# Summed squares ahead of the norm statistics, and a reordered end, in a two-layer hybrid backbone step on eight cores

## The chip, the cores and the metric

The kernel runs on all 8 cores of one Trainium2 chip, with one program and different data on each core. The metric is the device time of the slowest core in microseconds. In slow runs some cores, mostly of one die, run at a lower granted TensorE clock, and the time is longer.

## The reference

One inference step of a two-layer network. Layer 0 mixes tokens with gated linear attention and a Fourier transform, layer 1 with a chunked gMLP and a short convolution. Each layer has two modulated RMS norms and a squared-ReLU feed-forward. A final RMS norm ends it. Cut to what matters here:

```python
def rmsnorm(x, g):
    xf = x.astype(jnp.float32)
    y = xf * lax.rsqrt(jnp.mean(xf * xf, axis=-1, keepdims=True) + EPS)
    return (y * g.astype(jnp.float32)).astype(x.dtype)

for l in range(DEPTH):                      # DEPTH = 2, D = 1024, D_FF = 4096
    ...                                     # six modulation vectors from the conditioning
    h = rmsnorm(x, norm_mix_g[l]) * (1.0 + sc_m) + sh_m
    y = even_mixer(h, ...) if l % 2 == 0 else odd_mixer(h, ...)
    x = x + g_m * y
    h = rmsnorm(x, norm_ffn_g[l]) * (1.0 + sc_f) + sh_f
    x = x + g_f * (jnp.square(jax.nn.relu(h @ ffn_w1[l])) @ ffn_w2[l])
return rmsnorm(x, final_norm_g), outs_f, outs_b
```

## The kernel before

A core holds 1536 tokens as three blocks of 512: blocks 0 and 1 are one request's latent tokens, block 2 is context. The residual `xT[m]` has the 1024 features as 8 chunks of 128 partitions and the 512 tokens as columns. The mean of squares over features therefore crosses partitions, and it is made on TensorE: each chunk is squared on ScalarE (ACT) and multiplied by a matrix of constants, and eight such matmuls add up in one PSUM bank.

```python
def norm_stats(m, x):
    ps = PT(R)
    for c in range(8):
        sq = ring(sqr)
        act(sq[:], x[:, c, :], AF.Square, [x[:, c, :]], [sq[:]])
        R.add("pe", [(lambda sq=sq, c=c: nc.tensor.matmul(ps.f(), onesb[:], sq[:],
                      start=(c == 0), stop=(c == 7)), [sq[:], onesb[:]], 216)], W=[ps])
    r = ring(rsr)
    act(r[:], lambda: ps.f(), AF.Ln, ...)          # r = exp(-0.5 * ln(mean + eps))
    act(r[:], r[:], AF.Exp, ..., scale=-0.5)
    return r

def norm(l, wh, m):
    r = norm_stats(m, xT[m])
    for c in range(8):
        nt = ring(ntr)
        ...   # VectorE: nt = x * gain * r;  ACT: hT[m][:, c] = nt + shift
```

The second feed-forward product takes its weights in four pieces `u` of two output chunks each. The last pieces run block by block, each block followed by its final norm and eight stores:

```python
    if half == 1:                                   # inside ffn(l, hooks)
        for m in range(NM):
            for u in (2, 3):
                for o2 in range(2):
                    ffn2(l, ws[u], u, o2, m)        # 16 matmuls, then x += gate * psum on VectorE
            yield m
...
for m in ffn(1, lambda k: None):
    r = norm_stats(m, xT[m])
    for c in range(8):
        ys = ring(ysr)                              # 7 buffers of [128, 512]
        ...                                         # VectorE: ys = x * gain * r
        store(y_d[m, c], ys[:], "dys%d" % i, 128 * 2048)
```

Instructions are not issued in the order of this text. The program records them and a list scheduler orders each engine's queue by priority. `bl` is the estimated length of the work that depends on an operation, so an edit at the end changes the order of everything ahead of it:

```python
o.prio = o.seq - 1e7 if o.dma is not None and o.eng == "pool" else 30.0 * o.seq - o.bl
```

```python
wO = [w8("evO%d" % i, wevo_d[i]) for i in range(2)]   # weights of the layer-0 output projection, gpsimd queue
xload(0, "sp", 6, 8)
xload(1, "sp")                                        # reload of block 1's input, sync queue
...
for m in range(NM):                                   # gMLP, layer 1
    ...                                               # projections to u and v, 512 columns each
    for jj in range(4):
        for g in range(4):                            # two matmuls of 128 columns: W_s v, and the bias
            ...
        ...                                           # VectorE: mixc = psum * u
```

## Time and profile before

| Kernel before | us |
|---|---|
| median time, first 4 runs | 1202.56 (1200.47 to 1202.95) |
| span of the slowest core in the profile | 1201.7 |
| TensorE busy | 1120.7 (93%) |
| VectorE / ACT / GpSimd busy | 454.1 / 425.0 / 106.0 |

To compare versions I cut every core's profiled run at two landmarks, the starts of the first and of the last matmul of the second feed-forward product (the groups whose tiles are `aT` and `w_f`). This gives a head, a stretch that TensorE bounds, and a tail, averaged over the eight cores. For the kernel before they are 409.6, 768.6 and 20.5 us.

### The profile page before, as it was taken

How to read it: one execution, taken by the hardware profiler on the slowest of the kernel's cores; microseconds unless marked ns; L12 is line 12 of the kernel's file. 1: busy time of each engine (PE TensorE's matmuls, PEld its weight loads, DVE VectorE, ACT ScalarE, POOL GpSimd, SP SyncE). 2: the span in 40 equal slices, each digit the busy share in tenths (PEclk: the TensorE clock that was granted, in tenths of full speed). 3: DMA queues.
4: the chain of work that ended last, by engine and by line, in shares of the span. 5: the costliest groups of instructions: out<-in, count | busy, mean ns of one | idle time of the engine just before them, and what ended most of it. 6: DMA issues, size and time to landing. Idle time of an engine off the chain costs nothing.

```text
span 1201.7 us, 15088 instructions; the slowest of 8 cores (1195.1 to 1201.7 us)
## 1 busy us (share of the span) xinstructions
PE 1120.7 (93%) x6242; PEld 533.5 (44%) x6242; DVE 454.1 (38%) x894; ACT 425.0 (35%) x764; POOL 106.0 (9%) x193
## 2 busy tenths in 40 slices
PE   2479999979989999999999999999999999999994
PEld 0234555644434444444444444444444444444441
DVE  1248476866532222222223514445522222222226
ACT  2473768535553200122113732243733000232013
POOL 2004144520000000000000000000000000000000
PEclk9989999899989999999999989999999999999998
DMA  9980132898951813356333801035232014420005
GB/s 185 229 160 1 23 75 44 153 225 145 193 102 36 140 36 71 70 106 117 71 58 65 148 1 31 6 71 98 43 55 52 5 31 82 88 41 1 1 1 210
DMA packets 19057, 98.19 MB, mean 82 GB/s; under 512 B 2123, under 2 KB 5451, under 8 KB 9132
## 3 DMA queue, kind: packets, MB, share of 16 engines
q0 software_dynamic: 11312, 82.12, 37.9%
q1 hardware_dynamic: 5372, 13.53, 3.5%
q10 hardware_dynamic: 2304, 1.57, 0.4%
q8 instruction: 49, 0.80, 0.3%
q14 instruction: 20, 0.16, 0.1%
HBM read 165.17 MB, written 7.86 MB: 144 GB/s over the span
## 4 chain that ended last, share of the span: by engine, by line
PE 83%; DMA 6%; DVE 4%; ACT 4%; issue 1%; POOL 1%; ACTq 0%; DVEq 0%; POOLq 0%
PE ps L475 80%; DMA w_evC<-wevc 3%; DMA w_evO<-wevo 3%; ACT hA L485 2%; PE ps L1077 1%; PE ps L583 1%; DVE nt L597 1%; DVE ys L1145 1%; ACT sq L485 1%; ACT rstd L485 0%; DVE RS L834 0%; DVE xT L604 0%; DVE hA L877 0%; ACT relu L485 0%; DVE og L866 0%
## 5 line engine op out<-in xcount | busy, mean ns | idle before, releaser
L475 PE MATMUL ps<-hA,w_f 128*128 128x512 bf16 x1536 | 344.9, 382 | 3.0 <-ACT hA L485 2.8
L475 PE MATMUL ps<-aT,w_f 128*128 128x512 bf16 x1536 | 339.7, 379 | 0.0
L485 ACT ACTIVATE relu<-ps 128x512 bf16<-128x512 f32 x192 | 114.1, 596 | 407.3 <-PE ps L475 407.3
L475 PEld LDWEIGHTS ps<-hA,w_f 128*128 128x128 bf16 x1536 | 150.0, 98 | 187.7 <-ACT hA L485 8.6
L475 PEld LDWEIGHTS ps<-aT,w_f 128*128 128x128 bf16 x1536 | 150.3, 98 | 180.9
L604 DVE SCALAR_TENSOR_TENSOR xT<-ps,modT,xT 128x512 f32<-128x512 f32 x144 | 108.0, 751 | 285.0 <-PE ps L475 284.6
L1008 DVE TENSOR_TENSOR aT<-relu 128x512 bf16<-128x512 bf16 x192 | 81.7, 426 | 254.3 <-ACT relu L485 254.1
L485 ACT ACTIVATE sq<-xT 128x512 bf16<-128x512 f32 x120 | 71.7, 623 | 180.7 <-PE ps L583 113.8
L485 ACT ACTIVATE hA<-nt,modT 128x512 bf16<-128x512 f32 x96 | 65.9, 717 | 39.7 <-DVE nt L597 39.3
L597 DVE SCALAR_TENSOR_TENSOR nt<-xT,gsc,rstd 128x512 f32<-128x512 f32 x96 | 68.3, 751 | 17.6 <-ACT rstd L485 13.7
L475 PE MATMUL ps<-w_vg,hA 128*128 128x512 bf16 x288 | 67.0, 380 | 0.9 <-DVE att L849 0.5
L583 PE MATMUL ps<-sq,ones 128*128 128x512 bf16 x120 | 45.1, 401 | 24.1 <-ACT sq L485 22.5
L497 POOL DMA_DIRECT2D w_f<-wf x32 | 17.0, 531 | 430.1 <-PE ps L475 363.9
L475 PE MATMUL ps<-hA,w_evO 128*128 128x512 bf16 x176 | 43.8, 399 | 5.9 <-DMA w_evO<-wevo 5.9
L475 PE MATMUL ps<-hA,w_qk 128*128 128x512 bf16 x192 | 45.3, 379 | 1.4 <-issue 0.6
L819 POOL TENSOR_SCALAR sprevS<-RS,dec 128x192 bf16<-128x192 f32 x56 | 44.3, 801 | 18.4 <-DVE RS L834 16.9
L475 PEld LDWEIGHTS ps<-w_vg,hA 128*128 128x128 bf16 x288 | 27.0, 98 | 30.4 <-issue 1.4
L497 POOL DMA_DIRECT2D w_ada<-wada x20 | 10.8, 540 | 231.2 <-PE ps L475 224.8
L583 PEld LDWEIGHTS ps<-sq,ones 128*128 128x128 bf16 x120 | 11.6, 98 | 42.4 <-ACT sq L485 19.6
L475 PEld LDWEIGHTS ps<-hA,w_evO 128*128 128x128 bf16 x176 | 17.7, 102 | 27.3 <-DMA w_evO<-wevo 6.4
L475 PEld LDWEIGHTS ps<-hA,w_qk 128*128 128x128 bf16 x192 | 17.7, 98 | 20.6 <-issue 1.1
L485 ACT ACTIVATE t<-ps 128x1024 f32<-128x1024 f32 x24 | 23.9, 1023 | 7.9 <-PE ps L475 7.9
(155 smaller groups left out, 932.2 us busy)
## 6 DMA issues: line engine op xcount, KB each, us to landing
w_f<-wf POOLq DMA_DIRECT2D x32, 1024.0 KB, 8.2
w_ada<-wada POOLq DMA_DIRECT2D x20, 1024.0 KB, 10.1
xT<-x POOLq DMA_DIRECT2D x3, 2048.0 KB, 52.3
y<-ys SPq DMA_DIRECT2D x24, 256.0 KB, 2.8
w_ada_s<-wada POOLq DMA_DIRECT2D x4, 1024.0 KB, 27.8
xT<-x SPq DMA_DIRECT2D x2, 2048.0 KB, 23.7
w_vg<-wev POOLq DMA_DIRECT2D x3, 1024.0 KB, 48.3
w_qk<-wev POOLq DMA_DIRECT2D x2, 1024.0 KB, 46.6
```

Source lines behind the costliest of these rows:

```text
L475: parts.append((lambda view=view, l=l, r=r, i=i, n=n: nc.tensor.matmul(view(), l, r, start=(i == 0), stop=(i == n - 1)), [l, r], max(27.0, ...
L485: R.add("act", [(lambda: nc.scalar.activation(out=o(), in_=i(), func=func, **kw), Rd, dur)], W=W, tab=tab)
L497: R.add(q, [(lambda: h.dma_start(out=dst, in_=src), [], 1000 if q == "pool" else 100)], W=[dst], dma=(key, nbytes), prio=prio)
L583: R.add("pe", [(lambda sq=sq, c=c: nc.tensor.matmul(ps.f(), onesb[:], sq[:], start=(c == 0), stop=(c == 7)), [sq[:], onesb[:]], 216)], W=[ps])
L597: lambda nt=nt, c=c: nc.vector.scalar_tensor_tensor(out=nt[:], in0=x[:, c, :], scalar=gsc[l][:, wh, c, ci:ci + 1], in1=r[:], op0=ALU.mult, ...
L604: lambda: nc.vector.scalar_tensor_tensor(out=x[:, oc, :], in0=ps.f(), scalar=modT[l][:, gch + oc, CI(m):CI(m) + 1], in1=x[:, oc, :], op0=A ...
L819: lambda d=d, j=j, pj=pj: nc.gpsimd.tensor_scalar_mul(sprev(d, j), Rt[d][:], dc[:, d, pj:pj + 1]), eng="pool")
L1008: vop(2, [a], [rl[:]], lambda a=a, rl=rl: nc.vector.tensor_tensor(out=a, in0=rl[:], in1=rl[:], op=ALU.mult))
L1077: parts.append((lambda g=g, l_=l_, r_=r_, i=i, p=p: nc.tensor.matmul(p.f(g * 128, (g + 1) * 128), l_, r_, start=(i == 0), stop=(i == 1)), ...
L1145: lambda ys=ys, c=c, m=m, r=r: nc.vector.scalar_tensor_tensor(out=ys[:], in0=xT[m][:, c, :], scalar=pp[:, PP_GF + c:PP_GF + c + 1], in1=r[ ...
```

## The change

Two intents. First, add the eight squared chunks on engines that are free (three adds on GpSimd, four on VectorE) so that one matmul with the constants replaces eight. This is done in seven norms (layer 0's second norm of block 2, all six of layer 1) and in the final norms. Second, shorten the work after the last matmul: block 1 goes ahead of block 2's last four chunks, these run in two halves of 256 columns, output chunks are stored in pairs, and a `bonus` moves priorities. The diff, cut to its core:

```diff
-            o.prio = ... else 30.0 * o.seq - o.bl
+            o.prio = ... else 30.0 * o.seq - o.bl - o.bonus
@@ norm statistics
+        def sq_sum(m, x, accs, n):
+            af, ab = ring(accs[0]), ring(accs[1])          # fp32 partial sum, bf16 result
+            s0 = sq_chunk(x, 0)
+            for c in range(1, n):
+                s1 = sq_chunk(x, c)
+                acc_add((ab if c == n - 1 else af)[:], (s0 if c == 1 else af)[:], s1[:], "pool" if c < 4 else "dve")
+            return ab
@@
+            if accs is None:
                 ...                                         # eight matmuls, as before
+            else:
+                ab = sq_sum(m, x, accs, 8)
+                mm(ps, [(lambda: ps.f(), [(onesb[:], ab[:])])])
@@
-        norm(0, 1, 2)
+        norm(0, 1, 2, accs0)                                # and accs1 for the six norms of layer 1
@@ order of the last feed-forward matmuls
+            if l == 1:
+                k = "a" if u < 2 and m == 2 else "b" if u >= 2 and m == 1 else ("lo" if lo == 0 else "hi") if ... else None
+                if k:                                       # each stage waits for the one before
+                    stages.setdefault(k, []).append(o)
+                    o.parts[0][1].update(stages.get({"a": "-", "b": "a", "lo": "b", "hi": "lo"}[k], ()))
@@ the end
+            for c in range(0, 8, 2):                        # final(m, r, lo, hi): chunks in pairs
+                ...
+                store(y_d[m, c:c + 2, :, lo:hi]..., "act" if m == 2 and c % 4 else "sp")
@@
+        for lo in (0, 256):
+            hi = lo + 256
+            R.bonus = 10000.0 if lo == 0 else 0.0
+            ps = PT(R)
+            mm(ps, [(... [(onesb[:], ab[:, lo:hi])])], stop=False)   # chunks 0 to 3, summed before
+            for c in range(4, 8):
+                ffn2(1, w2last[c // 2], c // 2, c % 2, 2, lo, hi)
+                ...                                         # square and statistics of this chunk
+            rstd_of(ps, r, lo, hi)
+            R.bonus = 0.0
+            final(2, r, lo, hi)
```

More of the change, by code (lines that the diff above doesn't have):

```diff
@@ L41 @@
     __slots__ = ("eng", "parts", "seq", "prio", "tab", "lat", "dma", "newpt", "pts",
-                 "succ", "npred", "bl", "extt", "tag", "ext", "ready", "start", "fin", "key", "val", "dur")
+                 "bonus", "succ", "npred", "bl", "extt", "tag", "ext", "ready", "start", "fin", "key", "val", "dur")
 class Rec:
@@ L60, in __init__ @@
         self.tag = None
+        self.bonus = 0.0
     def sb(self, name, shape, dt, off):
@@ L98, in add @@
         o.tag = self.tag
+        o.bonus = self.bonus
         o.pts = []
@@ L167, in schedule @@
         for o in ops:
-            o.prio = o.seq - 1e7 if o.dma is not None and o.eng == "pool" else 30.0 * o.seq - o.bl
+            o.prio = o.seq - 1e7 if o.dma is not None and o.eng == "pool" else 30.0 * o.seq - o.bl - o.bonus
         cand = {e: [] for e in self.ENGS}
@@ L467, in is_ps, with mm @@
             return isinstance(a, PT)
-        def mm(p, groups, pre=()):
+        def mm(p, groups, stop=True):
             parts = []
@@ L474, in mm @@
                 for i, (l, r) in enumerate(prs):
-                    parts.append((lambda view=view, l=l, r=r, i=i, n=n: nc.tensor.matmul(view(), l, r, start=(i == 0), stop=(i == n - 1)),
+                    parts.append((lambda view=view, l=l, r=r, i=i, n=n: nc.tensor.matmul(view(), l, r, start=(i == 0), stop=(stop and i == n - 1)),
                                   [l, r], max(27.0, nfree(r) / 2.4 + 2.5)))
@@ L574, in CI, with sq_chunk, acc_add, rstd_of @@
             return 0 if m == 2 else 1
-        def norm_stats(m, x):
+        def sq_chunk(x, c):
+            sq = ring(sqr)
+            act(sq[:], x[:, c, :], AF.Square, [x[:, c, :]], [sq[:]])
+            return sq
+        def acc_add(o_, a_, b_, eng):
+            e_ = nc.gpsimd if eng == "pool" else nc.vector
+            vop(1, [o_], [a_, b_], lambda: e_.tensor_tensor(out=o_, in0=a_, in1=b_, op=ALU.add), eng=eng, pool1=False)
+        def sq_sum(m, x, accs, n):
[5 more added lines that the diff above has]
+            return ab
+        def rstd_of(ps, r, lo, hi):
+            act(r[:, lo:hi], lambda: ps.f(lo, hi), AF.Ln, [ps, cst[:]], [r[:, lo:hi]], tab="nle", bias=cst[:, 0:1])
+            act(r[:, lo:hi], r[:, lo:hi], AF.Exp, [r[:, lo:hi]], [r[:, lo:hi]], tab="nle", scale=-0.5)
+        def norm_stats(m, x, accs=None):
             R.tag = "stats%d" % m
             ps = PT(R)
-            parts = []
-            for c in range(8):
-                sq = ring(sqr)
-                act(sq[:], x[:, c, :], AF.Square, [x[:, c, :]], [sq[:]])
-                R.add("pe", [(lambda sq=sq, c=c: nc.tensor.matmul(ps.f(), onesb[:], sq[:], start=(c == 0), stop=(c == 7)), [sq[:], onesb[:]], 216)], W=[ps])
+            if accs is None:
+                for c in range(8):
+                    sq = sq_chunk(x, c)
+                    R.add("pe", [(lambda sq=sq, c=c: nc.tensor.matmul(ps.f(), onesb[:], sq[:], start=(c == 0), stop=(c == 7)), [sq[:], onesb[:]], 216)], W=[ps])
+            else:
+                ab = sq_sum(m, x, accs, 8)
+                mm(ps, [(lambda: ps.f(), [(onesb[:], ab[:])])])
             r = ring(rsr)
-            act(r[:], lambda: ps.f(), AF.Ln, [ps, cst[:]], [r[:]], tab="nle", bias=cst[:, 0:1])
-            act(r[:], r[:], AF.Exp, [r[:]], [r[:]], tab="nle", scale=-0.5)
+            rstd_of(ps, r, 0, 512)
             return r
-        def norm(l, wh, m):
+        def norm(l, wh, m, accs=None):
             R.tag = "norm%d%d%d" % (l, wh, m)
@@ L592, in norm @@
             shc = 0 if wh == 0 else 24
-            r = norm_stats(m, x)
+            r = norm_stats(m, x, accs)
             for c in range(8):
@@ L599, in norm, with resid @@
                 act(h[:, c, :], nt[:], AF.Identity, [nt[:], modT[l][:, shc + c, :]], [h[:, c, :]], bias=modT[l][:, shc + c, ci:ci + 1])
-        def resid(m, oc, ps, l, gch):
-            x = xT[m]
-            vop(1, [x[:, oc, :]], [ps, x[:, oc, :], modT[l][:, gch + oc, :]],
-                lambda: nc.vector.scalar_tensor_tensor(out=x[:, oc, :], in0=ps.f(), scalar=modT[l][:, gch + oc, CI(m):CI(m) + 1], in1=x[:, oc, :],
+        def resid(m, oc, ps, l, gch, lo=0, hi=512):
+            x = xT[m][:, oc, lo:hi]
+            vop(1, [x], [ps, x, modT[l][:, gch + oc, :]],
+                lambda: nc.vector.scalar_tensor_tensor(out=x, in0=ps.f(lo, hi), scalar=modT[l][:, gch + oc, CI(m):CI(m) + 1], in1=x,
                                                        op0=ALU.mult, op1=ALU.add))
@@ L657, in build @@
         y256 = R.sb("y256", [128, 2, 128], BF16, a_s + 16384)
+        a_t4 = so[0]
         t4 = [R.sb("t4_%d" % i, [128, 1024], F32, ats(4096)) for i in range(4)]
@@ L983, in build @@
         outproj(0, wO, hT, 1)
+        accs0 = ([R.sb("af0_%d" % i, [128, 512], F32, a_t4 + i * 2048) for i in range(2)],
+                 [R.sb("ab0_%d" % i, [128, 512], BF16, a_t4 + 4096 + i * 1024) for i in range(2)])
         norm(0, 1, 0)
@@ L989, in build @@
         norm(0, 1, 1)
-        norm(0, 1, 2)
+        norm(0, 1, 2, accs0)
         aT = [R.sb("aT%d" % m, [128, 16, 512], BF16, a_s + m * 16384) for m in range(NM)]
         a_s2 = a_s + 49152
+        accs1 = ([R.sb("af1_%d" % i, [128, 512], F32, a_s2 + 12288 + i * 2048) for i in range(2)],
+                 [R.sb("ab1", [128, 512], BF16, a_s2 + 16384)])
+        assert a_s2 + 17408 <= s_end
         def ffn(l, hooks):
@@ L1015, in ffn @@
                         for m in range(NM):
+                            R.bonus = 0.0 if half == 0 or l == 0 else 0.0
                             for o2 in range(2):
                                 ffn2(l, w, u, o2, m)
+                        R.bonus = 0.0
                     hooks((half, 1, u))
                 if half == 1:
-                    for m in range(NM):
+                    w2last.update({2: ws[2], 3: ws[3]})
+                    for m in range(NM if l == 0 else 2):
+                        R.bonus = 0.0 if l == 0 else 0.0
                         for u in (2, 3):
@@ L1023, in ffn, with ffn2 @@
                                 ffn2(l, ws[u], u, o2, m)
+                        R.bonus = 0.0
                         yield m
-        def ffn2(l, w, u, o2, m):
+        w2last = {}
+        stages = {}
+        def ffn2(l, w, u, o2, m, lo=0, hi=512):
             p = PT(R)
-            mm(p, [(lambda: p.f(), [(w[:, kc, o2 * 128:(o2 + 1) * 128], aT[m][:, kc, :]) for kc in range(16)])])
-            resid(m, u * 2 + o2, p, l, 40)
+            o = mm(p, [(lambda: p.f(lo, hi), [(w[:, kc, o2 * 128:(o2 + 1) * 128], aT[m][:, kc, lo:hi]) for kc in range(16)])])
+            if l == 1:
+                k = "a" if u < 2 and m == 2 else "b" if u >= 2 and m == 1 else ("lo" if lo == 0 else "hi") if u >= 2 and m == 2 and hi - lo < 512 else None
+                if k:
+                    stages.setdefault(k, []).append(o)
+                    o.parts[0][1].update(stages.get({"a": "-", "b": "a", "lo": "b", "hi": "lo"}[k], ()))
+            resid(m, u * 2 + o2, p, l, 40, lo, hi)
         def hooks0(k):
@@ L1036, in build @@
         for m in ffn(0, hooks0):
-            norm(1, 0, m)
+            norm(1, 0, m, accs1)
         cload(wsT[:], gws_d, "pool")
@@ L1129, in build @@
         oproj1(0, mds[0])
-        norm(1, 1, 0)
+        norm(1, 1, 0, accs1)
         mds.append(gh(2))
         oproj1(1, mds[1])
-        norm(1, 1, 1)
+        norm(1, 1, 1, accs1)
         oproj1(2, mds[2])
-        norm(1, 1, 2)
-        so[0] = a_s2
-        ysr = [R.sb("ys%d" % i, [128, 512], F32, ats(2048)) for i in range(7)]
-        for m in ffn(1, lambda k: None):
-            r = norm_stats(m, xT[m])
-            for c in range(8):
-                ys = ring(ysr)
-                i = (cnt[id(ysr)] - 1) % 7
-                vop(1, [ys[:]], [xT[m][:, c, :], r[:], pp[:]],
-                    lambda ys=ys, c=c, m=m, r=r: nc.vector.scalar_tensor_tensor(out=ys[:], in0=xT[m][:, c, :], scalar=pp[:, PP_GF + c:PP_GF + c + 1],
-                                                                                in1=r[:], op0=ALU.mult, op1=ALU.mult))
-                store(y_d[m, c], ys[:], "dys%d" % i, 128 * 2048)
+        norm(1, 1, 2, accs1)
@@ new lines, in build, with final @@
+        ysr = [R.sb("ys%d" % i, [128, 2, 512], F32, a_h + i * 4096) for i in range(6)]
+        def final(m, r, lo, hi):
+            for c in range(0, 8, 2):
+                ys = ring(ysr)
+                i = (cnt[id(ysr)] - 1) % 6
+                for c_ in (c, c + 1):
+                    o_, x_, g_ = ys[:, c_ - c, 0:hi - lo], xT[m][:, c_, lo:hi], pp[:, PP_GF + c_:PP_GF + c_ + 1]
+                    if False:
+                        vop(1, [o_], [x_, pp[:]], lambda o_=o_, x_=x_, g_=g_: nc.gpsimd.tensor_scalar_mul(o_, x_, g_), eng="pool")
+                        vop(1, [o_], [o_, r[:, lo:hi]], lambda o_=o_: nc.gpsimd.tensor_tensor(out=o_, in0=o_, in1=r[:, lo:hi], op=ALU.mult),
+                            eng="pool", pool1=False)
+                    else:
+                        vop(1, [o_], [x_, r[:, lo:hi], pp[:]], lambda o_=o_, x_=x_, g_=g_: nc.vector.scalar_tensor_tensor(
+                            out=o_, in0=x_, scalar=g_, in1=r[:, lo:hi], op0=ALU.mult, op1=ALU.mult))
+                store(y_d[m, c:c + 2, :, lo:hi].rearrange("c p t -> p c t"), ys[:, :, 0:hi - lo], "dys%d" % i, 128 * (hi - lo) * 8,
+                      "act" if m == 2 and c % 4 else "sp")
@@ new lines, in build @@
+        ab2 = [R.sb("ab2", [128, 512], BF16, R.base[ntr[0].name][0])]
+        for m in ffn(1, lambda k: None):
+            if m < 2:
+                R.bonus = [20000.0, 20000.0][m]
+                r = norm_stats(m, xT[m], accs1)
+                R.bonus = [20000.0, 0.0][m]
+                final(m, r, 0, 512)
+            if m == 0:
+                R.bonus = 0.0
+                ab = sq_sum(2, xT[2], (accs1[0], ab2), 4)
+            R.bonus = 0.0
+        r = ring(rsr)
+        for lo in (0, 256):
+            hi = lo + 256
+            R.bonus = 10000.0 if lo == 0 else 0.0
+            ps = PT(R)
+            mm(ps, [(lambda ps=ps, lo=lo, hi=hi: ps.f(lo, hi), [(onesb[:], ab[:, lo:hi])])], stop=False)
+            for c in range(4, 8):
+                ffn2(1, w2last[c // 2], c // 2, c % 2, 2, lo, hi)
+                sq = ring(sqr)
+                act(sq[:, 0:256], xT[2][:, c, lo:hi], AF.Square, [xT[2][:, c, lo:hi]], [sq[:, 0:256]])
+                R.add("pe", [(lambda sq=sq, c=c, ps=ps, lo=lo, hi=hi: nc.tensor.matmul(ps.f(lo, hi), onesb[:], sq[:, 0:256], start=False, stop=(c == 7)),
+                              [sq[:, 0:256], onesb[:]], 110)], W=[ps])
+            rstd_of(ps, r, lo, hi)
+            R.bonus = 0.0
+            final(2, r, lo, hi)
```

## The prediction

> **What bounds the kernel now.** I first read the engine shares and the row of forty slices on the page of the profile.
>
> ```profile
> PE 1120.7 (93%) x6242; PEld 533.5 (44%) x6242; DVE 454.1 (38%) x894; ACT 425.0 (35%) x764; POOL 106.0 (9%) x193
> ...
> PE   2479999979989999999999999999999999999994
> ```
>
> TensorE (PE) is the bound, except in the head, in the slices with 7 and 8 and in the last slice. A busy PE may still be one that waits, so the second view is busy time by stretch, for the slowest core (1), then the same stretch for the matmuls of the norm statistics alone (L583, ones times a squared chunk).
>
> ```profile
> 345.00:1182.00 837.00, 835.55 (x4170) 383.33 (x4168) 248.39 (x436) 225.82 (x372) 23.22 (x44) 0.99 0.32 58
> 1182.00:1202.00 20.00, 4.38 (x14) 1.05 (x11) 11.45 (x17) 7.20 (x13) 0.00 (x0) 0.70 0.55 210
> ...
> 345.00:1182.00 837.00, 21.92 (x60) 5.97 (x61) 0.99 0.32 58
> ```
>
> The columns after the length are PE, PE weight load, DVE, ACT and POOL, busy us and count, then the granted clock. From 345 to 1182 us PE idles 1.45 us of 837 at clock 0.99, while DVE and ACT work under a third of the time: whatever leaves PE's queue here comes off the span, and 60 of its matmuls are statistics. In the last 20 us PE has almost nothing. What one statistics matmul costs is read from PE's timeline:
>
> ```profile
> 1141.70 0.38 PE L583 MATMUL ps<-sq,ones 128*128 128x512 bf16 x1
> 1141.92 3.62 PE L475 MATMUL ps<-aT,w_f 128*128 128x512 bf16 x16
> 1145.37 0.38 PE L583 MATMUL ps<-sq,ones 128*128 128x512 bf16 x1
> 1145.59 3.62 PE L475 MATMUL ps<-aT,w_f 128*128 128x512 bf16 x16
> ```
>
> The 0.38 us overlaps its neighbours; the place in the queue is from 1145.37 to 1145.59, 0.22 us, and sixteen others take 3.45. Last, the end in the timeline and the head in the list of waits, the chain and the timeline:
>
> ```profile
> 1178.61 3.62 PE L475 MATMUL ps<-aT,w_f 128*128 128x512 bf16 x16
> ...
> 1182.27 0.75 DVE L604 SCALAR_TENSOR_TENSOR xT<-ps,modT,xT 128x512 f32<-128x512 f32 x1 [1.89 <-PE ps L475]
> 1182.48 3.75 ACT L485 ACTIVATE sq<-xT 128x512 bf16<-128x512 f32 x7 [3.04 <-PE ps L583]
> ...
> 1187.94 10.69 DVE L1145 SCALAR_TENSOR_TENSOR ys<-xT,pp,rstd 128x512 f32<-128x512 f32 x16 [4.93 <-ACT rstd L485]
> ```
>
> ```profile
> PE ps L475 <- DMA w_evO<-wevo: 5.9, 1, 5.9
> ...
> 234.65 34.58 DMA w_evO<-wevo
> ...
> 269.27 9.95 PE L475 MATMUL ps<-hA,w_evO 128*128 128x512 bf16 x32 [5.92 <-DMA w_evO<-wevo]
> ```
>
> The tail is from the last feed-forward matmul, 1182.2, to 1201.7: 19.5 us. Squares and statistics of two token blocks are crowded into it, DVE waits 4.93 us for the reciprocal root, then makes 16 output chunks in 10.69 us (0.67 each), and 3.1 us pass from its end (1198.6) to the end of the span, for the last store. In the head PE waits 5.9 us for the second half of the output projection's weights.
>
> [...] here eight of 128x256 in the head take 0.87 us, so halving costs nothing. [...] a granted clock of 0.54 and 0.61 in the two 4 us stretches after the 5.9 us wait, where 32 matmuls took 9.95 us in place of 6.9. [...]
>
> **The change, part by part.** (1) Seven norms and the final norms of blocks 0 and 1 first add their eight squared chunks, three adds on POOL and four on DVE, the last into bf16, so that one ones-matmul serves in place of eight. The order of the built program shows this: layer 0's second norm for block 2 and all six of layer 1, one matmul each. In the PE-bound stretch the 60 become: six norms 6, final norms of blocks 0 and 1 2, first four chunks of block 2 (two halves) 1, first half of its last four 2: 11 in units of 512 columns. 49 x 0.2157 = 10.6 us off PE. The price is 9 x 4 = 36 DVE adds, at up to 0.7 us some 25 us on an engine with 590 us free, and 9 x 3 plus 3 for block 2's first four chunks = 30 POOL adds[...] on an engine busy 23 us of 837.
>
> (2) The tail. Block 1 runs before the second half of block 2, and block 2's last four chunks run in two halves of 256 columns (lo, then hi), so only hi's work should follow the last feed-forward matmul, whose end I call e. [...] After e: 0.2 to the residual, 0.4 for it; in the built DVE order six lo chunks follow (2.4), then eight hi chunks (3.2), a sum of 6.2. ACT's queue has two store issues between the hi half's steps, so I add about 0.5 for the hi root coming late, and the same 3.1 for the last store: 9.8 us. In place of 19.5 that is 9.7 us off.
>
> (3) The head is reordered, though no work there changes but block 2's statistics (7 fewer, 1.5 us): priorities are computed back from the end. In the new PE order 23.3 us of work (summed by kind at the pitches of this trace) plus small gaps, about 24, lie between the last DFT matmul (233.2) and the first use of the late weights, where 30 lay before. The load itself is limited by a DMA that is busy 1.0 throughout 232 to 292, behind two other loads on its queue (its issue moves from 234.7 to about 240, with the load ahead of it still landing until 248), so I expect it at 269 again: PE waits about 12 us, not 6. In turn the next wait shrinks: only 32 feed-forward matmuls come ahead of block 2's projection in place of 48, which leaves 16 + 32 around its one statistics matmul, though about 4 us of waiting for its normed chunks remain. The old order lost 0.8 us near 310 and about 3 near 335. Also, block 0's eighth statistics matmul now stands about 24 us behind the late weights (plus 3 for the cold clock), so its eight normed chunks (0.75 us apiece with DVE's evictions between) end near 308, where PE began this feed-forward at 301. Followed through to where PE runs freely (341 before), I come to 343: 2 us lost.
>
> Sum: -10.6 - 9.7 + 2 = -18.3; 1202.6 - 18.3 = 1184.
>
> **The rivals.** First, POOL and DVE adds become the wait: a norm's root now stands behind add after add, and weight-load issues stand behind POOL adds in the same in-order queue. For it: each last add lengthens the chain by 0.6 to 0.7 us; the output-projection weights of layer 1 are issued after six adds. Against it: between the last matmul of a block and its statistics the new order has 16 to 32 other matmuls (3.45 to 6.9 us), against some 2.7 us for residual, square and add, and 40 more matmuls (8.6 us) follow before the last block's chunks are needed. If it bites at each of the seven norms by 1 us, 1191.
>
> Second, the head: if the late weights stall PE 12 us and nothing is given back, the head loses 7 to 9 and the time is 1190. If the load lands earlier, because two others no longer queue right behind it, the head gains 3 to 4: 1179.
>
> Third, the tail is bound by DVE: in the last 14 us before e it has block 1's eight chunks (5.4), eight half residuals (3.2) and some adds. By my count it runs about 1 us behind PE at e. If POOL or ACT hold it up more, the tail is 12 and the time 1187. A fourth, that the removed statistics matmuls were hidden in waits, is refuted by the 1.45 us of PE idling.
>
> **Range and chances.** The PE saving is the safest term (10 to 11), the tail within 2, the head within 6 either way, unforeseen waits 0 to 5. That gives 1184 us, 1176 to 1192 at 8 in 10. Faster by over 2% needs under 1178.5: only with a gain in the head, 0.16. Slower by over 2% has hardly a way, 0.01; within 2%, 0.83.
>
> **What would show it.** Right: about 10 or 11 statistics matmuls' worth of PE time where 60 were; feed-forward groups back to back, without 0.22 us steps; from the last feed-forward matmul to the end 9 to 11 us; a longer wait for the output projection's second weights, 10 to 13 us, with PE running freely near 343. Wrong: PE waits in layer 1 on the summed square or the root; [...] weight loads issued late behind them; DVE far behind PE at the last matmul; or the late weights landing well away from 269.

The 0.2157 us for a statistics matmul's place, used in the expectations too, is also what the trace of the kernel before shows: 32 matmuls of 512 columns stand from 711.50 to 718.40 us, 0.2156 us each. The tail's 2.4 and 3.2 us count six and eight half-size products at 0.40 us each; that was my estimate, and it had no trace of such a product behind it.

## The result, and the profile after

The changed kernel took 1179.61 us (median of 10 runs, of which three were slow), beside 1201.89 us for the kernel before (15 runs) on the same chip. The ratio of fast runs is 0.9812, with a 95% interval of 0.9802 to 0.9822: 1.9% faster, just inside the two per cent that count as the same. A ratio here is the mean time of one kernel's fast runs over that of the other's of the same rounds, so it is not quite the ratio of the medians. The prediction of 1184 was 4.4 us too high, within its range.

The page of the profile after, engine shares and TensorE's row of forty slices:

```profile
PE 1104.3 (94%) x6245; PEld 533.6 (45%) x6245; DVE 482.7 (41%) x942; ACT 429.2 (36%) x770; POOL 144.5 (12%) x223
...
PE   2479999989999999999999999999999999999997
```

TensorE's busy time fell by 16.4 us, VectorE's and GpSimd's grew by 28.6 and 38.5 us, and the last slice shows 7 tenths where it showed 4. Next, busy time by stretch on the slowest core (again core 1), with the same columns as in the prediction:

```profile
345.00:1168.00 823.00, 822.16 (x4223) 384.97 (x4222) 279.62 (x482) 237.05 (x388) 58.74 (x72) 1.00 0.34 63
1168.00:1178.00 10.00, 0.76 (x6) 0.28 (x3) 6.58 (x17) 1.31 (x3) 0.00 (x0) 0.68 0.66 225
```

The stretch in which TensorE runs freely shortened from 837 to 823 us. TensorE idles 0.84 us of it, and its clock reads 1.00 instead of 0.99. The window behind it shortened from 20 to 10 us. The sums that paid for this, by form:

```profile
L585 DVE TENSOR_TENSOR af<-af,sq x27: 676/689/693, 326.3 to 1151.5; 128x512 f32<-128x512 f32 x27
L585 POOL TENSOR_TENSOR af<-af,sq x19: 1143/1155/1641, 322.0 to 1141.2; 128x512 f32<-128x512 f32 x19
L585 POOL TENSOR_TENSOR af<-sq,sq x10: 1142/1149/2181, 320.3 to 1134.2; 128x512 f32<-128x512 bf16 x10
L585 DVE TENSOR_TENSOR ab<-af,sq x9: 680/692/694, 330.6 to 1154.9; 128x512 bf16<-128x512 f32 x9
L585 POOL TENSOR_TENSOR ab<-af,sq x1: 1153/1153/1153, 1131.5 to 1131.5; 128x512 bf16<-128x512 f32 x1
```

The three numbers are the shortest, median and longest in ns. There are 36 adds of 0.69 us on VectorE and 30 of about 1.15 us on GpSimd, in counts what the prediction worked out; VectorE's are near the 0.7 us that it allowed. The tail in the timeline:

```profile
1166.24 1.91 PE L477 MATMUL ps<-aT,w_f 128*128 128x256 bf16 x16
...
1168.48 0.48 DVE L629 SCALAR_TENSOR_TENSOR xT<-ps,modT,xT 128x256 f32<-128x256 f32 x1
...
1168.87 2.46 DVE L1194 SCALAR_TENSOR_TENSOR ys<-xT,pp,rstd 128x256 f32<-128x256 f32 x6
...
1171.52 3.25 DVE L1194 SCALAR_TENSOR_TENSOR ys<-xT,pp,rstd 128x256 f32<-128x256 f32 x8 [0.19 <-ACT rstd L487]
```

The last feed-forward matmul ends at 1168.15 us. Then follow the last residual, six products that were left over, eight of the second half at 0.41 us each, and 2.4 us to the end of the span at 1177.2. Before, sixteen products of 0.67 us stood there. From start to start that is 0.66 us ((10.69 − 0.75) / 15, with 0.75 for the last one) and for the halves 0.40 ((3.25 − 0.48) / 7), so a product costs about 0.13 us plus 0.53 us for each 512 columns. Last, the head: TensorE's waits from 225 to 345 us, and two lines of its timeline.

```profile
PE ps L477 <- ACT hA L487: 5.4, 11, 0.9
PE ps L477 <- DMA w_evO<-wevo: 2.7, 1, 2.7
PE ps L477 <- DVE xT L629: 2.0, 1, 2.0
PE ps L898 <- DVE hA L903: 1.5, 2, 0.9
```

```profile
268.34 6.37 PE L477 MATMUL ps<-hA,w_evO 128*128 128x512 bf16 x16 [2.71 <-DMA w_evO<-wevo]
...
308.00 7.25 PE L477 MATMUL ps<-hA,w_f 128*128 128x512 bf16 x25 [0.60 <-ACT hA L487]
```

In the list of waits the numbers are the sum in us, the count and the longest. The late weights landed at 268.3, near the predicted 269, but the wait was 2.7 us, not 12. The feed-forward was fed freely from 308.0, as predicted.

Where the time went, as means over the eight cores:

| us | head | TensorE-bound stretch | of it lost at half clock | tail | span |
|---|---|---|---|---|---|
| before | 409.6 | 768.6 | 7.5 | 20.5 | 1198.7 |
| after | 409.6 | 755.0 | 4.7 | 9.5 | 1174.1 |
| difference | 0.0 | −13.6 | −2.8 | −11.0 | −24.6 |
| predicted | +2 | −10.6 | not considered | −9.7 | −18.3 |

These are single executions, the profiled ones. The record has the cores' spans for other runs too: over fast runs their mean is 1197.8 us before (21 runs of the later sessions) and 1174.8 after (8 runs), which is 23.1 us less and not 24.6. Those 21 runs are of other chips. So some 1.5 us of the difference in the span may be chance between executions or chips.

What was open at this point: whether the 2.8 us of half-clock time belong to the sums, what sets these half-clock stretches, what each part of the tail is worth, and why the head cost nothing.

### The profile page after: what moved, and what is told of

It reads as the page before. It is cut to its first block, busy times and chain, and to the rows that moved or that the text cites. A ratio compares the mean times of both kernels' runs of the same rounds, so it can differ in the third digit from the quotient of the medians.

```text
span 1177.2 us, 15132 instructions; the slowest of 8 cores (1170.1 to 1177.2 us)
## 1 busy us (share of the span) xinstructions
PE 1104.3 (94%) x6245; PEld 533.6 (45%) x6245; DVE 482.7 (41%) x942; ACT 429.2 (36%) x770; POOL 144.5 (12%) x223
## 4 chain that ended last, share of the span: by engine, by line
PE 86%; DMA 6%; DVE 5%; ACT 2%; issue 1%; POOL 1%; DVEq 0%; POOLq 0%; ACTq 0%
PE ps L477 84%; DMA w_evC<-wevc 3%; DMA w_evO<-wevo 2%; DVE nt L622 2%; PE ps L1121 1%; ACT hA L487 1%; DVE xT L629 1%; DVE ys L1194 1%; ACT rstd L487 0%; DVE RS L860 0%; ACT sq L487 0%; PE ps L606 0%; DVE hA L903 0%; DVE af L585 0%; DVE att L875 0%
## 5 line engine op out<-in xcount | busy, mean ns | idle before, releaser
L477 PE MATMUL ps<-aT,w_f 128*128 128x512 bf16 (+1 forms) x1600 | 339.2, 370 | 0.0
L477 PEld LDWEIGHTS ps<-aT,w_f 128*128 128x128 bf16 x1600 | 156.3, 98 | 174.8
L629 DVE SCALAR_TENSOR_TENSOR xT<-ps,modT,xT 128x512 f32<-128x512 f32 (+1 forms) x148 | 108.5, 735 | 249.6 <-PE ps L477 247.0
L487 ACT ACTIVATE sq<-xT 128x512 bf16<-128x512 f32 (+1 forms) x124 | 73.7, 612 | 167.9 <-DVE xT L629 135.2
L606 PE MATMUL ps<-sq,ones 128*128 128x512 bf16 x40 | 16.2, 437 | 20.6 <-ACT sq L487 19.9
L585 POOL TENSOR_TENSOR af<-af,sq 128x512 f32<-128x512 f32 x19 | 24.1, 1267 | 66.8 <-ACT sq L487 66.4
L487 ACT ACTIVATE junk<-ps 128x192 bf16<-128x192 f32 x48 | 15.8, 330 | 40.1 <-PE ps L477 39.8
```

Of the source, the lines that this page charges most:

```text
L477: parts.append((lambda view=view, l=l, r=r, i=i, n=n: nc.tensor.matmul(view(), l, r, start=(i == 0), stop=(stop and i == n - 1)), [l, r], ...
L487: R.add("act", [(lambda: nc.scalar.activation(out=o(), in_=i(), func=func, **kw), Rd, dur)], W=W, tab=tab)
L585: vop(1, [o_], [a_, b_], lambda: e_.tensor_tensor(out=o_, in0=a_, in1=b_, op=ALU.add), eng=eng, pool1=False)
L629: lambda: nc.vector.scalar_tensor_tensor(out=x, in0=ps.f(lo, hi), scalar=modT[l][:, gch + oc, CI(m):CI(m) + 1], in1=x, op0=ALU.mult, op1=A ...
```

## The experiments

Ten kernels ran, each in five rounds against the kernel before. All results were correct. Before's medians in the three sessions were 1204.33, 1202.79 and 1202.36 us, so ratios are the safe comparison. They are of fast runs alone, while the medians given include slow runs: two each in e1_sums_only, e2_tail_only and e9_whole_ordered, one in e6_mix_spread, four in e3_eight_again and three in e5_adds_dve. Head, stretch and tail are means of the one profiled execution of each.

**e1_sums_only**: the kernel before with the sums in the seven norms and nothing else.

```diff
-            for c in range(8):  ...                # eight matmuls with ones
+                ab = sq_sum(m, x, accs, 8)
+                mm(ps, [(lambda: ps.f(), [(onesb[:], ab[:])])])
-        norm(1, 1, 0)
+        norm(1, 1, 0, accs1)                       # likewise the other six
```

> The kernel before plus the summed statistics in the seven norms only; final norms and tail as before. Theory: 42 of the removed matmuls lie in the PE-bound stretch, 42 x 0.2157 = 9.1 us off PE, and the half-clock stretches of layer 1 (14.9 us per core before, 9.4 after) shrink with it, another 2 to 3 us; the tail stays at 20.5 us from the start of the last feed-forward matmul. So 1190 us, ratio 0.990. If the shorter half-clock stretches come from something else (the reordering by the tail's priorities), 1193. Rival, adds on POOL and DVE become waits: 1196 or more.

Measured: 1190.79 us, ratio 0.9898 (0.9883 to 0.9914). Head 410.0, stretch 756.5 (4.9 of it lost at half clock), tail 19.9. The sums alone give 12.1 of the stretch's 13.6 us, with the smaller half-clock loss, and nothing of the tail.

**e2_tail_only**: the changed kernel with eight matmuls again in the seven norms.

```diff
-        norm(1, 1, 0, accs1)
+        norm(1, 1, 0)                              # likewise the other six
```

> The changed kernel with eight statistics matmuls again in the seven norms; tail and final norms as changed. Theory: the tail stays at 9.5 us (11.0 less than before), the final norms' own saving of some 7 matmuls (1.5 us) stays, the 9.1 us of the seven norms come back, and with them the half-clock stretches near 14.9 us: 1189 to 1190 us, ratio to before 0.990. If the clock gain belongs to the tail's reordering, 1187. If the parts are not additive (the tail gains only because of the sums elsewhere), 1195.

Measured: 1191.95 us, ratio 0.990 (0.9879 to 0.9921). Spans and mean granted clocks by core:

```profile
core 1: 1183.7 us, clock 0.984
core 2: 1208.0 us, clock 0.946
core 3: 1208.1 us, clock 0.958
core 4: 1185.6 us, clock 0.967
```

Cores 2 and 3 show mean granted clocks of 0.946 and 0.958, the six others 0.965 to 0.984, and their spans are over 20 us longer than the others' (1183.7 to 1188.0 us), so they are left out. On the six others the tail is 9.3 to 9.5 us and the stretch 766.8 to 768.4, with 6.8 to 8.5 us lost at half clock, as in the kernel before. The tail's gain therefore needs no sums in the seven norms. The two gains of 1.0% each add up to 2.0%, within the intervals of the whole 1.9%.

**e3_eight_again**: the changed kernel, in which each sum is multiplied eight times by a matrix of ones, accumulated, and scaled back. The adds stay and the matmuls come back.

```diff
-                mm(ps, [(lambda: ps.f(), [(onesb[:], ab[:])])])
+                mm(ps, [(lambda: ps.f(), [(cb[:, 896:1024], ab[:])] * 8)])
-            rstd_of(ps, r, 0, 512)
+            rstd_of(ps, r, 0, 512, 1.0 if accs is None else 1.0 / 8192)
```

> The changed kernel with every sum multiplied eight times into the same accumulator (ones of 1.0 and a scale of 1/8192 in the logarithm, so the result stays right): adds, waits and order stay, only the matmuls come back, 56 of them in the PE-bound stretch and 7 in the head. Theory (the gain is places in PE's queue): 56 x 0.2157 = 12.1 us slower than the changed kernel, 1191.5 us. Rival (the gain is fewer waits between ScalarE's squares and PE): within 2 us of the changed kernel, 1180 to 1182.

Measured: 1215.71 us median of seven runs, of which four were slow. The ratio of fast runs is 0.9951 (0.9928 to 0.9974), about 1196 us. The stretch grew by 12.0 us to 767.0, close to the expected 12.1. But 1.5 us of it is more half-clock loss, and 0.8 us of waits on the summed square are gone (core 1), so the 56 matmuls themselves made about 11.3. So a statistics matmul taken out of the queue is worth about its place there, and the rival, a gain of fewer waits, is out. The head missed: it grew by 5.9 us, not 1.5. The scheduler had reordered it, and TensorE waited 10.6 us for the late weights (7.8 to 10.8 on the eight cores), close to the wait that I had predicted for the changed kernel:

```profile
PE ps L477 <- DMA w_evO<-wevo: 10.7, 2, 10.6
```

**e6_mix_spread**: what the half-clock stretches follow. In the kernel before, the timeline of TensorE around 700 us shows 32 gMLP matmuls of 128 columns in one run, without idling:

```profile
698.36 0.22 PE L1077 MATMUL ps<-wsT,v 128*128 128x128 bf16 x1
698.51 0.23 PE L1077 MATMUL ps<-gbr,cb 33*128 33x128 bf16 x1
...
703.88 0.29 PE L1077 MATMUL ps<-gbr,cb 33*128 33x128 bf16 x1
704.09 5.84 PE L475 MATMUL ps<-w_odV,hA 128*128 128x512 bf16 x16
709.77 1.89 PE L475 MATMUL ps<-hA,w_odGb 128*128 128x512 bf16 x8
```

From 698.36 to 704.09 they start every 0.16 us (at the end every 0.22). In the head, matmuls of 128 columns start every 0.06 us (four from 246.27 to 246.44 us). The records have half clock from 701.8 to 708.6. Then sixteen matmuls of 512 columns take 5.68 us from start to start where sixteen others take 3.45 (0.43 us each up to 708.3, 0.22 from 708.7 on), and from 709.77 on the usual 1.73 for eight is back. The half-clock stretches recorded in the TensorE-bound stretch of both kernels last 3.4 us or twice that. TensorE counts as busy here, though these matmuls start nearly three times as far apart as those in the head. That their runs set the half-clock stretches was my guess at this point. The changed kernel keeps these runs, so the guess promised a version faster than both: put each eight of them behind a projection of eight 512-column matmuls of the next block (for the last block, of a later product), by an ordering dependency.

```diff
+        prev = None
+        chain = [None]
         for m in range(NM):
             ...
-                proj(p, wU, oc * 128, hT, m)
+                o = proj(p, wU, oc * 128, hT, m)
+                if prev and oc:
+                    o.parts[0][1].add(chain[0])
+                if prev:
+                    gmix(prev[0], oc, prev[1], prev[2], o)   # the 8 small matmuls of the block before
-            for jj in range(4):  ...                         # 32 small matmuls in one run
+            prev = (m, u_, v_)
```

> The changed kernel with the spatial-gating matmuls of layer 1 (128x128, half of them with 33 rows, 32 in a run of 5 us) spread in eights between projections of 512 columns. Theory (the half-clock stretches of layer 1 follow these runs[...]): the half-clock stretches of layer 1 go from 9.4 us per core to 0 to 3, and the time falls by 3 to 4.7 us, to 1175 to 1176.5. Rival (the stretches come from waits or by chance): the stretches stay near 9 us and the time within 1.5 us of 1179.6.

Measured: 1174.86 us, ratio 0.9768 (0.9752 to 0.9783), faster than both kernels. Busy time by stretch of the kernel before, of the changed kernel (both core 1), then of this one (core 0, its slowest), with the clock behind POOL's count:

```profile
700.00:740.00 40.00, 40.00 (x180) 18.26 (x180) 14.01 (x21) 9.33 (x15) 0.00 (x0) 0.87 0.00 0
```

```profile
690.00:730.00 40.00, 40.00 (x189) 18.59 (x188) 13.01 (x20) 11.59 (x21) 0.00 (x0) 0.91 0.00 1
```

```profile
690.00:730.00 40.00, 39.79 (x193) 18.56 (x196) 7.02 (x10) 10.72 (x18) 0.00 (x0) 1.00 0.01 2
```

In all three, TensorE is busy practically all the time, but the clock is 0.87, 0.91 and 1.00. On all eight cores no half-clock time is left in the stretch, which is 750.7 us: 4.3 less than in the changed kernel, against 4.7 lost there. The runs of small matmuls cause these stretches. Which of their properties does it (128 columns, 33 rows in every second one, the 0.16 us pitch) was not separated. The head was 2.9 us longer in this profile, though TensorE's matmuls stand in it in the changed kernel's order. The other four fast runs have mean spans 1.0 to 3.1 us shorter than the profiled one, so this is mostly variation between executions.

**e4_no_halves**: the changed kernel with block 2's last four chunks in one piece.

```diff
-        for lo in (0, 256):
-            hi = lo + 256
+        for lo in (0,):
+            hi = 512
```

> The changed kernel with block 2's last four output chunks normalized in one piece of 512 columns again instead of two halves of 256; the new order of the blocks, the paired stores and the sums stay. If the halves are worth what the sum of the tail says (the last statistics and the last eight products on 256 columns instead of 512, products at a pitch of 0.41 us instead of about 0.7, less the second statistics chain), the stretch from the start of the last matmul of the second feed-forward product to the end should be about 2.2 us longer, 11.6 instead of 9.4, and the time about 1182. If the order of the blocks and the stores carry the whole 11 us of the tail, the time stays at 1179.6 within 0.5.

Measured: 1189.54 us, ratio 0.9887 (0.9873 to 0.99), tail 19.8 us, far more than 11.6. The timeline shows why:

```profile
1170.98 0.57 PE L477 MATMUL ps<-ab,ones 128*128 128x512 bf16 x1 [2.02 <-DVE ab L585]
...
1172.97 10.69 DVE L1194 SCALAR_TENSOR_TENSOR ys<-xT,pp,rstd 128x512 f32<-128x512 f32 x16 [2.04 <-ACT rstd L487]
```

Block 1's statistics came after the last feed-forward matmuls, so sixteen output products stood at the end again. The dependency that puts block 1 ahead is tied to pieces under 512 columns, and the one piece kept the bonus of the first half. My edit had lost the order too, and the run does not test the halves.

**e9_whole_ordered**: as before, but without the bonus; in the built order block 1 stands ahead again.

```diff
-            R.bonus = 10000.0 if lo == 0 else 0.0
+            R.bonus = 0.0
```

> As the run without halves before it, but with no priority bonus on block 2's last four chunks, so that in the built order block 1 stands whole ahead of them, as in the changed kernel. That run had its statistics of block 1 behind the last feed-forward matmuls and so 16 output products after them, tail 19.8 us: it tested a lost order, not the halves. Here, after the last feed-forward matmul, follow residual 0.75, square 0.63, statistics 0.4, logarithm 0.69, exponential 0.63, eight products at 0.67 (5.35), the last store 3.1, a sum of 11.6, and up to two products of block 1 that are left over (1.3). So if order and halves are separate terms the tail is 11.6 to 13 us in place of 9.4 and the time 1182 to 1183.5. If the order alone carries the whole gain of the tail, it is 9.4 and 1179.6; if the halves carry it, 19 to 20 and 1189.

Measured: 1182.19 us, ratio 0.9831 (0.9816 to 0.9847), tail 13.1 us, head and stretch as in the changed kernel.

```profile
1170.78 0.63 ACT L487 ACTIVATE rstd<-rstd 128x512 f32<-128x512 f32 x1
1171.51 5.39 DVE L1194 SCALAR_TENSOR_TENSOR ys<-xT,pp,rstd 128x512 f32<-128x512 f32 x8 [2.66 <-ACT rstd L487]
```

Eight products of 0.67 us remain. Of the tail's 11.0 us, the order with the paired stores and the final norms' sums, which were not separated, makes 7.4 (20.5 to 13.1), and the halves with their bonus 3.6 (13.1 to 9.5).

**e5_adds_dve**: the changed kernel with all adds on VectorE.

```diff
-                acc_add((ab if c == n - 1 else af)[:], ..., s1[:], "pool" if c < 4 else "dve")
+                acc_add((ab if c == n - 1 else af)[:], ..., s1[:], "dve")
```

> The changed kernel with all seven adds of each sum on VectorE, none on GpSimd. My theory: the sums lie beside TensorE work in the PE-bound stretch, so the place of the adds costs nothing there; VectorE gets 21 to 33 more adds of 0.4 to 0.7 us and has some 60 per cent of the stretch free: time within 1 us of 1179.6. Rival, that GpSimd's adds slow VectorE's reads and hold the norms back: 1 to 3 us faster. Second rival, that a longer serial chain of adds on VectorE holds a norm back where its output is needed at once: 1 to 3 us slower, with new waits of TensorE on the normalized tile.

Measured: 1183.79 us median of eight runs, three of them slow; ratio 0.9833 (0.982 to 0.9846), so about 2.5 us slower than the changed kernel by the ratios. The profiled run, the fastest of its kernel, doesn't show that loss: its mean span is 1174.4 us against 1174.1, where the other four fast runs have 1175.7 to 1178.3. It shows 7.0 us of half-clock loss in place of 4.7, while the rest of the stretch is 1.8 us shorter. TensorE's two waits on the summed square (0.8 us) are gone, and no new wait stands there. VectorE's norm products take 747 ns on average, against 769 with GpSimd's adds beside them and 751 in the kernel before; in all runs with the sums' adds on GpSimd it is 761 to 770, in those with few or none 747 to 751. Why was not shown. The expected tie within 1 us was missed by the times, and neither rival was seen in the records. The edit also reordered TensorE's matmuls in the head. Whether the half-clock stretches make the whole difference is not decided by this run.

**e7_reload_queued**: the changed kernel with block 1's reload queued behind the late weights.

```diff
-        xload(1, "sp")
+        xload(1, "pool")
```

> The changed kernel with block 1's reload of the input issued on the same queue as the second half of the weights of the layer-0 attention output, behind it, instead of on a queue of its own beside it. If the late landing of that half (268.3 us, TensorE waits 2.7 us for it, and a half-clock stretch follows) is the sharing of the 16 DMA engines with the reload, it lands at 258 to 262, the wait and the stretch near 267 go, and the time is 2 to 4 us shorter, about 1176. Rival: the half is late for its own size; it lands at 265 or later and the time stays within 0.5 us. Second rival: what is gained is lost again to the reload or the feed-forward weights landing later, with a new wait of TensorE between 270 and 345.

Measured: 1176.05 us, ratio 0.9776 (0.9763 to 0.9789), about 4 us faster than the changed kernel by the ratios, which come from two sessions; the mean spans of fast runs differ by 2.4 us (1172.4 and 1174.8). By the profiles' means the head is 2.2 us shorter. TensorE's waits on core 1 from 225 to 345 us:

```profile
PE ps L477 <- DVE xT L629: 1.8, 1, 1.8
...
PE ps L477 <- DMA w_evO<-wevo: 0.4, 1, 0.4
```

The 0.4 us here is a wait for the first half of the weights, at 247.3 us. For the late half TensorE waits 0.2 to 2.9 us on the eight cores of the changed kernel, and on none of this one. On core 1 it landed at 263.2 us in place of 268.3. About 1.9 us of this is an earlier issue, which the edit did not make, since no engine's order differs before 242 us. The time from issue to landing fell from 26.8 to 23.6 us; on the eight cores it was 25.0 to 26.9 us and is 22.4 to 24.4. So the weights took longer beside a load on a queue of its own than ahead of one on theirs. How the two loads shared the DMA engines was not shown. The landing came later than my 258 to 262, so part of the lateness is the load's own.

**e8_spread_queued**: both edits, e6_mix_spread and e7_reload_queued.

> The changed kernel with both the gMLP matmuls spread between the projections (e6_mix_spread, ratio 0.9768 to the kernel before) and the reload queued behind the second half of the weights (e7_reload_queued). The two act in different stretches (345 us to the end, and 225 to 345), so if both are what I hold them for they add: about 1171 to 1173. If the queued reload gives nothing it stays at e6's 1175; if it stalls TensorE, 1177.

Measured: 1171.51 us, ratio 0.9735 (0.9721 to 0.9748). Head 407.8, stretch 750.8 with no half-clock loss, tail 9.4. The two add up.

**e10_spread_queued_dve**: that version with all adds on VectorE, to see the place of the adds without the half-clock stretches.

> The version with spread gMLP matmuls and the queued reload (1171.5) with all adds of the sums on VectorE. The changed kernel with all adds on VectorE came out about 2.5 us slower than the changed kernel by the ratios; its records show 7.0 us instead of 4.7 us of half-clock loss per core in the PE-bound stretch and no new wait there. If that is all the place of the adds does, it does nothing where the half-clock stretches of layer 1 are gone: the same ratio as the version with both, 0.9735, within 0.1 per cent. If the adds on VectorE hold the norms back themselves, it is 2 to 3 us slower again, 0.9755.

Measured: 1167.45 us, ratio 0.9719 (0.9704 to 0.9733), the fastest version: 2.8% below the kernel before. Neither expectation holds exactly: by the ratios it is 0.16% faster than e8_spread_queued, with intervals that overlap, and by the mean spans of fast runs 4.1 us (1163.1 and 1167.2). Adds on VectorE that hold the norms back are ruled out. The stretch is 1.3 us shorter (749.5), 0.8 of it the two waits on the summed square. The head is 3.7 us shorter (404.1); TensorE's order in it is another. It trades one set of waits for another (core 1, 225 to 345 us):

```profile
PE ps L477 <- DMA w_ada<-wada: 3.7, 1, 3.7
PE ps L477 <- DVE hA L903: 1.4, 4, 0.6
```

The waits on ACT's normed chunks, 5.4 us in the changed kernel, are no longer on the list of this core. So most of this gain is the head's new order, and not what the adds themselves cost.

## Why the prediction was right or wrong, point by point

**TensorE's queue: right, but the term was mis-sized because one effect was left out.** The step "49 x 0.2157 = 10.6 us off PE" is confirmed: net of half-clock time the stretch fell from 761.1 to 750.3 us, by 10.8 (0.6 of it fewer waits, by core 1), and e3_eight_again got 12.0 back by putting 56 matmuls in again (about 11.3 of it theirs). What the sum didn't have is that the half-clock loss fell too, from 7.5 to 4.7 us per core. e1_sums_only (4.9) and e2_tail_only (6.8 to 8.5 on undisturbed cores) tie this to the sums, and e6_mix_spread shows that runs of small matmuls carry such stretches. Why the new order leaves fewer of them is only partly seen: in the kernel before one stretch, near 860 us on three of the eight cores, follows waits of TensorE for normed chunks, 1.4 us in all on core 1, and in the changed kernel it is gone. For the others this stays open. I had read the clock of 0.99 in the stretch as full; on that core 8.5 us were in that 0.01.

**The tail: right in kind, 1.3 us too cautious.** By the prediction's own count, 9.8 us follow the last feed-forward matmul; on core 1 it was 9.1. The products have the predicted pitch (0.41 against 0.40) and the hi half's root did come late behind a store issue, by 0.65 us, of which VectorE lost 0.19. The last store took 2.4 us instead of 3.1, which is the term that was off. On core 1 the tail fell by 10.6 us by the landmarks and on the mean of the cores by 11.0; the rest of the 1.3 us lies in that and in counting from the last matmul's start, not its end. The rival "the tail is 12" did not come.

**The head: the net of +2 was 0.0 on the mean of the cores, and the step to it failed in one place.** That is "small gaps, about 24": I put TensorE at the late weights at about 257 us and had it wait 12. On core 1 it came there at 265.6. The last DFT matmul was at 235.5, not 233.2, and waits on VectorE that I had passed over as small gaps sum to about 4.8 us (0.18 to 1.97 us each); some 2 us are not accounted for. The landing (268.3) and the free start of the feed-forward (308.0) were as predicted, so less of the delay was waiting for the load and more was waiting before it. The wait of 12 us came on no core: it was 0.2 to 2.9 us on the eight, and 2.8 to 5.9 before. TensorE ran freely from 341.5, not 343. On this core, the slowest, the head was still 1.7 us longer than before, near the prediction; over the eight it was nothing. Part of that nothing may be chance: over all fast runs the mean span fell by 1.5 us less than in the profiled pair, and if stretch and tail are the same in the others, the head lost about 1.5 us there, near the predicted 2; this was not measured. e3_eight_again moved the head by +5.9, and e10_spread_queued_dve by −3.7 against e8_spread_queued, with edits that aim elsewhere but change TensorE's order in it; the +2.9 of e6_mix_spread came without a new order. So order and execution each move the head by some microseconds, and the prediction's ±6 for it was fair.

**The rivals.** GpSimd's and VectorE's adds as the new wait: TensorE waits 0.8 us on the summed square in all, not 1 us at each of seven norms. Weight-load issues did stand right behind adds (one add on GpSimd runs from 569.88 to 571.03 us, the issue of w_f behind it from 571.15), but TensorE waits for no weights from 345 us on. The load landing earlier, which alone would have given 1179: it did not land earlier, though e7_reload_queued shows that it could be made to. The time came to 1179.6 for other reasons, −2.8 of half clock, −2 in the head, −1.3 in the tail. These sum to 6.1, not 4.4; most of the rest is the 1.5 us by which the profiled pair differs more than the fast runs do on average.

## What to carry to other kernels

Where TensorE was the bound, summing operands on idle engines ahead of a reduction matmul was worth about the removed places in its queue (10.8 us for 10.6). The tail was worth as much again (11.0 us), once the last output was cut so that little follows the last matmul. Read the granted clock beside the busy share: here a busy TensorE that ran 32 small matmuls in a row fell to half clock for 3.4 or 6.8 us, and mixing them between large ones gave that back. When a list scheduler orders by priorities from the end, test an edit by its order too, since one that loses the order (here e4_no_halves) tests something else. Where one stretch varies between executions, as the head does here, look at the spans of several runs before a cause is named.
